# Hybrid decoder layer on one core: in the down product, the second sum's first pairs read into other tiles and in another place of the load order

## Chip, cores and metric

The kernel runs on 1 core of one Trainium2 chip. The metric is device time in microseconds (us). The kernel before has a median of 1271.38 us over three runs (1269.64 to 1272.08).

## The reference, cut to what matters

One decoder layer over 1024 tokens of width 1024: input projection, windowed attention beside a convolution branch, their gated mix, a layer norm, and then a ConvFFN. The change lies in the last matrix product, `@ ffn_w_down`, and in the start of what follows it:

```python
up = causal_dwconv(h @ ffn_w_up, ffn_dw, ffn_dw_b)
u, g = jnp.split(up, 2, axis=-1)
f = (jax.nn.gelu(g, approximate=False) * u) @ ffn_w_down
return layer_norm(DEEPNORM_ALPHA * h + f, ln2_g, ln2_b)
```

`gelu(g) * u` is 1024 x 2816 and `ffn_w_down` is 2816 x 1024, both float32.

## The kernel before, in words

**Number format.** A float32 product is computed as three passes: each operand is split into a rounded high half (a ScalarE copy, L1625) and the rest (a VectorE subtraction, L1626), and TensorE multiplies high by high, high by low and low by high.

**The up stage.** A loop over 22 chunks of 128 hidden columns computes `f`, transposed, and stores each chunk's two halves to the DRAM scratch `fd` (`f_out`, L1471 and the store behind it). The chain of the last half of a chunk is: a convolution (`conv_ffn`, L1461 to L1463), `gelu` on ScalarE (L1467), the multiplication on VectorE (L1471), the store. Temporaries of 128x512 come in rotation from eight places of the tile `FA` (`ftmp`); chunk 20 uses the first four, `FA[0:2048]`, the last chunk, 21, the next four, `FA[2048:4096]`. The tiles `c11`, `c21` and `u2` stand behind them in `FA`, `c12`, `c22` and `u13` in `OB[0:2048]`.

**The seven products.** The down product is done by Strassen and Winograd's scheme on 2 x 2 blocks: seven half-size products (the "sums" of the change's name are the accumulations), each over 11 slices of 128 hidden rows. Slices are taken in pairs, six to a product: five of two slices and one of a single slice. This document numbers the pairs 0 to 41: pairs 0 to 5 are the first product (A22 with T4, into the four accumulation banks `Z`, written `ps_z` in the profile), pairs 6 to 11 the second (A11 with B11, into `X`, `ps_x`), pairs 12 to 17 the third (S1 with T1, into `Z`), and so on. A pair of two slices is 24 matmuls of 128x512 (four banks, two slices, three passes), a single one 12. A11, A22 and A12 are blocks of `fd`; the third to sixth products read differences of blocks (S1 to S4), which lie in the DRAM scratch `sd`. `sd` is made chunk by chunk: `sums_load` reads two rows of chunks from `fd`, `sums_form` does four VectorE operations (L1501 to L1504) and stores the result in two transfers. For most chunks that happens within the up loop; the last two, 20 and 21 (`FC - 2` and `FC - 1`), are read and formed among the first pairs of the down product. Pair 16 reads what chunks 19 and 20 gave, pair 17 what chunk 21 gave. The T blocks lie in `td` and are finished long before.

**Buffers.** A pair has two raw tiles, one for the f side and one for the weight side. `F_RAW` has eight places: two in `RXF` (named `raw` in the profile), then six of 1024 columns in `FA`. `W_RAW` has six: two from a pool (`wr`), then `OB[2048:3072]`, `OB[3072:4096]`, `OB[0:1024]`, `OB[1024:2048]`. `place(i, n)` (L1608 to L1610) says which place pair i gets. The split halves of the f side have six places (`F_AT`), those of the weight side seven (`W_DN`), in rotation.

**Order.** All loads and stores of this stage are issued by SP, in program order: an instruction that waits holds up every later one. A transfer also waits for the landing of the one eight before it, because there are eight completion semaphores. `down_operands` yields pairs; `d_ahead` keeps six of them begun ahead of the product that is being emitted; `steps` (L1723) names the side work that is emitted after each pair: `gain_rows` (the norm's scale and shift rows, `w<-in_ln`), `row` (residual rows `r<-h1d`, scaled on VectorE at L1706 and L1707), `sums_load` and `sums_last`. From these a scheduler makes the order on each engine, within what `after` pins.

Of the kernel before, what the change touches and what calls it, by code (L numbers as in the profile page):

```python
# [44 lines left out]
FC = DFF // P  # L45
# [67 lines left out]
def tile_hybrid_layer(  # L113
# [9 lines left out]
    def load(o, i):  # L123
        return nc.sync.dma_start(out=o, in_=i)
# [5 lines left out]
    def f32(ap):  # L130
        return ap.bitcast(F)

    def after(ins, first):

        tc.add_manual_dep(ins.ins, first.ins.name, mybir.DependencyInfo(
            mybir.DependencyClass.NoSync, mybir.DependencyReason.SCHED_ONLY), reason="order of work")
# [159 lines left out]
    def wraw(shape):  # L296
        return wraw_p.tile(shape, F, name="wr", tag="wr")
# [479 lines left out]
    src = ps[:64, :P].rearrange("p (g d) -> p g d", d=HD)  # L777
    nc.scalar.copy(vm[:64, :, 0], src)
    nc.vector.tensor_tensor(vm[:64, :, 1], src, f32(vm[:64, :, 0]), OP.subtract)
    for q4 in range(2):  # L780
# [4 lines left out]
        src = ps[:, :].rearrange("p (n g d) -> p n g d", g=2, d=HD)  # L785
# [24 lines left out]
    for h in range(NH):  # L810
        g, r = divmod(h, 4)
        o = ps[:2, h * 16:(h + 1) * 16]
# [67 lines left out]
    for i in range(NB):  # L880
        w = 272 if i else 144
# [246 lines left out]
    for m in range(KC):  # L1128
# [38 lines left out]
        if m in (2, 3):  # L1167
            raw = (FA[:, 4112:5136], OB[:, 3072:4096])[m - 2]
# [426 lines left out]
    def blk(t, first, step, col):  # L1595
        return lambda j, n: dram(t, (first + j) * P * step + col, [[step, P], [P * step, n], [1, 512]])

    A11, A21, A12, A22 = (blk(fd, k, S, c) for k in (0, FH) for c in (0, 512))
    B11_, B12_, B21_, B22_ = (blk(w_down, k, D, c) for k in (0, FH) for c in (0, 512))
    T1, T3, T4, T2 = (blk(td, 0, 2048, q * 512) for q in range(4))  # L1600
    S2, S3, S4, S1 = (blk(sd, 0, 2048, q * 512) for q in range(4))

    F_AT = [(RHC, R_DN), (RX, 0), (RHC, 2048 + R_DN)] + [(RHO, i * 2048 + R_DN) for i in range(3)]
    W_DN = [(OC, OC_UP + i * 2048) for i in range(4)] + [(RHC, 4096 + R_DN), (RHC, 6144 + R_DN), (RHO, 6144 + R_DN)]
    F_RAW = [RXF[:, 0:1024], RXF[:, 1024:2048]] + [FA[:, i * 1024:(i + 1) * 1024] for i in range(6)]
    W_RAW = [None, None] + [OB[:, i * 1024:(i + 1) * 1024] for i in (2, 3, 0, 1)]

    def place(i, n):  # L1608

        return i % 4 if i < 6 else (i - 2) % n  # L1610
    PAIRS = [(j, min(2, FH - j)) for j in range(0, FH, 2)]

    los, evacs = [], []

    def operand(i, src, j, n, raws, places):
        raw = raws[place(i, len(raws))]
        if raw is None:
            raw = wraw([P, D])
        raw = raw[:, :n * 512]
        ins = load(raw.rearrange("p (n c) -> p n c", c=512), src(j, n))  # L1620
        after(ins, loads[-1] if loads else f_stores[-5])
        loads.append(ins)
        t, o = places[i % len(places)]
        hi, lo = (t[:, o + x:o + x + n * 512] for x in (0, 1024))
        nc.scalar.copy(hi, raw)  # L1625
        los.append(nc.vector.tensor_tensor(lo, raw, f32(hi), OP.subtract))  # L1626
        if len(los) > 1:
            after(los[-1], evacs.pop() if evacs else los[-2])
        return hi, lo

    def down_operands():
        i = 0
        for f, w in ((A22, T4), (A11, B11_), (S1, T1), (S2, T2), (S3, T3), (S4, B22_), (A12, B21_)):
            for j, n in PAIRS:
                yield (n,) + operand(i, f, j, n, F_RAW, F_AT) + operand(i, w, j, n, W_RAW, W_DN)
                i += 1

    d_stream, d_ready = down_operands(), []

    def d_ahead():  # L1640
        while len(d_ready) < 6:
            x = next(d_stream, None)
            if x is None:
                break
            d_ready.append(x)

    def d_next(ahead=True):
        if ahead:
            d_ahead()
        return d_ready.pop(0)  # L1650

    with rank(RK_SPLIT):
        d_ahead()

    def down(banks, first, done, by_tile=0, same=False):


        def mms(i, pairs, a, z):
            ops = [(p, c * 512) for p in pairs for c in range(p[0])]
            for x, ((n, fh, fl, wh, wl), o) in enumerate(ops):  # L1660
                ts, ws = slice(o + i * P, o + i * P + P), slice(o, o + 512)
                for k, (l, r) in enumerate(((fh, wh), (fh, wl), (fl, wh))):
                    nc.tensor.matmul(banks[i], l[:, ts], r[:, ws], start=first and a and x + k == 0,  # L1663
                                     stop=z and x == len(ops) - 1 and k == 2, skip_group_check=not first)

        n = len(PAIRS) - by_tile
        for y in range(n):
            p = d_next(y < 3 or not same)
            for i in range(4):
                mms(i, [p], y == 0, y == len(PAIRS) - 1)  # L1670
            if extra:
                extra.pop(0)()
        last = [d_next() for _ in range(by_tile)]
        for i in range(4):
            if last:
                mms(i, last, n == 0, True)
            with rank(RK_EVAC):
                ins = done(i)
        if same:
            evacs.append(ins)  # L1680
# [28 lines left out]
    def do(f, *x):  # L1709
        extra.append(lambda: f(*x))  # L1710
# [7 lines left out]
    def steps(*fs):  # L1718
        for f in fs:
            do(lambda f=f: [g(*x) for g, *x in f])  # L1720

    row = residual_row
    steps([(sums_load, FC - 2)], [(gain_rows, 0)], [(sums_last, FC - 2), (row, 4, 0)], [(row, 5, 0)], [(row, 6, 0)],  # L1723
          [(row, 7, 0), (sums_load, FC - 1)],
          [(row, 0, 0)], [(sums_last, FC - 1)], [(row, 1, 0)], [(row, 2, 0)], [(row, 3, 0)], [(row, 4, 1)],
          [(row, 5, 1)], [(row, 6, 1)], [(row, 7, 1)], [(row, 0, 1), (row, 1, 1)], [(row, 2, 1), (row, 3, 1)],
          [(gain_rows, 1)])
# [89 lines left out]
```

## Time and profile before

| what | value |
|---|---|
| median of three runs | 1271.38 us |
| time of the profiled execution | 1271.08 us |
| span of the profile | 1269.3 us (1.8 us of its time lie around the span) |
| TensorE granted clock over the span | 0.995 |
| VectorE, ScalarE busy | 85%, 47% |
| last matmul of the up stage to first of the down product | at 1047.4 us, without a gap |

A row of the timeline has the start in us from the span's beginning, the length, the engine, the source line, the operation, `out<-in`, shapes and a count; in brackets stands the idle time of that engine just before, and what ended it. PE is TensorE's matmul, PEld its weight load, DVE VectorE, ACT ScalarE, SPq the queue of SyncE, which issues transfers: the length of an SPq row is the time to issue, not to land. A row of several instructions spans all of them. A table by stretches gives the busy time and the count of each engine, the granted TensorE clock (1.00 is full speed), the busy share of the transfer engines and GB/s. Groups of transfers give the count, the size and the median time from issue to landing.

### The profile page before, as it was taken

To read this page: it belongs to the slowest core of one execution; us is meant where nothing else is said; L and a number is where in the kernel's file an instruction comes from. 1 tells how busy PE (TensorE), PEld (TensorE's weight loads), DVE (VectorE), ACT (ScalarE), POOL (GpSimd) and SP (SyncE) were. 2 spreads that over 40 slices of the span, in tenths; PEclk is the share of its full clock that TensorE was granted. 3 is DMA by queue.
4 is the path that set the end of the run, shared out by engine and by line. 5 is a ranking of instruction groups with operands and counts; after the bars stand their busy time and mean duration, and the time that the engine had idled before them with its cause. 6 is when DMAs were issued, how large, how long until landed. Compare 5 with 4: busy or idle time off the path is not lost.

```text
span 1269.3 us, 23031 instructions
## 1 busy us (share of the span) xinstructions
PE 1252.8 (99%) x9186; PEld 1184.5 (93%) x9186; DVE 1073.1 (85%) x1854; ACT 591.6 (47%) x1095; POOL 8.1 (1%) x9
## 2 busy tenths in 40 slices
PE   8999999999999999999999999999999999999997
PEld 7999999999999999788899999999999997788886
DVE  7888999999978577548999999998989975987697
ACT  7532355655473223335655455555554553535330
POOL 0000000001000000000000000000000000000000
PEclk9999999999999999999999999999999999999999
DMA  6375643332438364222245546454454566989712
GB/s 252 105 250 149 176 112 96 105 92 83 125 85 226 106 177 125 83 85 82 67 158 198 193 170 212 160 207 150 159 191 170 197 239 242 394 280 369 266 67 83
DMA packets 98701, 212.19 MB, mean 167 GB/s; under 512 B 11411, under 2 KB 38611, under 8 KB 98338
## 3 DMA queue, kind: packets, MB, share of 16 engines
q1 hardware_dynamic: 84474, 199.64, 47.3%
q10 hardware_dynamic: 14120, 11.08, 2.8%
q8 instruction: 72, 1.18, 0.4%
q14 instruction: 35, 0.29, 0.1%
HBM read 150.29 MB, written 62.70 MB: 168 GB/s over the span
## 4 chain that ended last, share of the span: by engine, by line
PE 93%; DVE 2%; DMA 2%; ACT 2%; issue 1%; SPq 0%; DVEq 0%; ACTq 0%
PE px L1534 14%; PE py L1534 10%; PE ps_x L1663 9%; PE ps_z L338 8%; PE ps_z L342 8%; PE ps_z L341 8%; PE pw L1534 5%; PE pz L1534 5%; PE ps_z L1663 5%; PE ps_p L342 2%; PE ps_p L338 2%; PE ps_p L341 2%; PE ps_w L342 2%; PE ps_w L338 2%; PE ps_w L341 2%; PE ps_z L556 2%
## 5 line engine op out<-in xcount | busy, mean ns | idle before, releaser
L342 PE MATMUL ps_z<-RHC,w 128*128 128x256 f32 (+2 forms) x864 | 244.6, 283 | 0.0
L338 PE MATMUL ps_z<-RHO,w 128*128 128x256 f32 (+2 forms) x864 | 244.4, 283 | 0.2 <-ACT FA L734 0.2
L341 PE MATMUL ps_z<-RHO,w 128*128 128x256 f32 (+2 forms) x864 | 243.2, 282 | 0.0
L338 PEld LDWEIGHTS ps_z<-RHO,w 128*128 128x128 f32 x864 | 162.6, 188 | 2.0 <-ACT FA L705 0.7
L341 PEld LDWEIGHTS ps_z<-RHO,w 128*128 128x128 f32 x864 | 162.7, 188 | 0.7
L342 PEld LDWEIGHTS ps_z<-RHC,w 128*128 128x128 f32 x864 | 162.7, 188 | 0.4
L725 DVE SCALAR_TENSOR_TENSOR FA<-cin,cdw,FA 128x1026 f32<-128x1026 f32 x120 | 152.3, 1279 | 0.7
L1356 DVE TENSOR_TENSOR RHO<-wr,RHO 128x512 fp32r<-128x512 f32 x94 | 63.5, 683 | 8.3 <-ACT RHO L1355 8.3
L1355 ACT CAST RHO<-wr 128x512 fp32r<-128x512 f32 x94 | 56.6, 619 | 23.2 <-DVE wr L1373 11.3
L300 ACT CAST w<-wr 128x1024 fp32r<-128x1024 f32 x37 | 38.7, 1046 | 60.8 <-PE ps_z L342 44.8
L734 ACT ACTIVATE FA<-ps_z,colr 128x258 f32<-128x258 f32 (+1 forms) x64 | 30.1, 472 | 69.8 <-PE ps_z L342 57.3
L1373 DVE TENSOR_TENSOR wr<-wr 128x512 f32<-128x512 f32 x88 | 60.0, 682 | 0.1
L303 DVE TENSOR_TENSOR w<-wr,w 128x1024 fp32r<-128x1024 f32 x37 | 45.0, 1217 | 16.3 <-ACT w L300 16.1
L1546 ACT COPY FA<-px 128x514 f32<-128x514 f32 (+2 forms) x23 | 13.1, 571 | 76.7 <-PE px L1534 76.7
L1356 DVE TENSOR_TENSOR w<-wr,w 128x512 fp32r<-128x512 f32 x60 | 40.6, 684 | 4.8 <-ACT w L1355 4.7
L1534 PE MATMUL px<-OA,RHO 128*128 128x258 f32 x324 | 43.2, 283 | 0.0
L1461 ACT ACTIVATE FA<-OB,coll 128x512 f32<-128x512 f32 x44 | 35.9, 815 | 15.0 <-DVE OB L1542 15.0
L1546 ACT COPY OB<-px 128x514 f32<-128x514 f32 (+2 forms) x46 | 26.2, 569 | 34.7 <-PE px L1534 34.5
L1534 PE MATMUL px<-RHC,RHO 128*128 128x258 f32 (+1 forms) x312 | 41.1, 281 | 0.4 <-ACT OB L1546 0.4
L1534 PE MATMUL px<-OC,RHO 128*128 128x256 f32 x324 | 41.5, 277 | 0.0
L1355 ACT CAST w<-wr 128x512 fp32r<-128x512 f32 x60 | 36.3, 618 | 11.1 <-DVE wr L1373 5.1
L1534 PEld LDWEIGHTS px<-OA,RHO 128*128 128x128 f32 x324 | 40.5, 189 | 0.2 <-ACT OB L1546 0.2
(442 smaller groups left out, 3297.2 us busy)
## 6 DMA issues: line engine op xcount, KB each, us to landing
wr<-in_w_up_dram SPq DMA_DIRECT2D x44, 512.0 KB, 3.6
wr<-in_w_z_dram SPq DMA_DIRECT2D x29, 512.0 KB, 3.7
fd<-FA SPq DMA_DIRECT2D x44, 256.0 KB, 2.1
OB<-in_w_down_dram SPq DMA_DIRECT2D x21, 512.0 KB, 4.8
FA<-sd SPq DMA_DIRECT2D x15, 512.0 KB, 9.0
qt<-qd SPq DMA_DIRECT2D x28, 256.0 KB, 4.1
sgd<-FA ACTq DMA_DIRECT2D x48, 128.0 KB, 2.7
td<-OB SPq DMA_DIRECT2D x12, 512.0 KB, 2.7
```

Source lines behind the costliest of these rows:

```text
L300: ins = nc.scalar.copy(hi, raw)
L303: return nc.vector.tensor_tensor(lo, raw, f32(hi), OP.subtract)
L338: ins = nc.tensor.matmul(ps, al, bh, start=i == 0, stop=False)
L341: nc.tensor.matmul(ps, ah, bh, start=False, stop=False)
L342: last = nc.tensor.matmul(ps, ah, bl, start=False, stop=i == n - 1)
L725: nc.vector.scalar_tensor_tensor(acc[c], cin[:, j:j + U], wc, acc[c], OP.mult, OP.add)
L1355: nc.scalar.copy(hi, src)
L1356: ins = nc.vector.tensor_tensor(lo, src, f32(hi), OP.subtract)
L1373: ins = nc.vector.tensor_tensor(*x)
L1534: ins = nc.tensor.matmul(o, x[:, ks], bmat(sub, q, hl, k), start=first and k + j == 0, stop=k == 3 and j == 2, skip_group_check=not first)
L1546: copied.append(nc.scalar.copy(*x))
L1663: nc.tensor.matmul(banks[i], l[:, ts], r[:, ws], start=first and a and x + k == 0, stop=z and x == len(ops) - 1 and k == 2, skip_group_che ...
```

## The change

`place` repeats its four places once more: pairs 6 and 7 get places 2 and 3 (`FA[0:2048]`, `OB[2048:4096]`), which pairs 2 and 3 had, in place of 4 and 5 (`FA[2048:4096]`, `OB[0:2048]`). Later pairs go round all places as before, two further on.

`operand` is cut in two: `operand_load` issues the transfer, `operand` does the split. In the list of pairs 5 and 6 change places: both are loaded when the fifth pair (pair 4) is reached, pair 6 first; then pair 6 is split before pair 5. The product still takes them by number.

In `steps`, chunk 20 is read three steps later (with residual row 5, after pair 3 instead of pair 0) and formed three steps later, after pair 5; chunk 21 is read in the same step as before and formed in the same step. The gain rows are still read in the second step, residual row 4 in the third.

```diff
     def place(i, n):

-        return i % 4 if i < 6 else (i - 2) % n
+        return i % 4 if i < 8 else (i - 4) % n
...
-    def operand(i, src, j, n, raws, places):
+    def operand_load(i, src, j, n, raws, places):
...
         loads.append(ins)
-        t, o = places[i % len(places)]
+        return raw, n, places[i % len(places)]
+
+    def operand(raw, n, at):
+        t, o = at
...
     def down_operands():
-        i = 0
-        for f, w in ((A22, T4), (A11, B11_), (S1, T1), (S2, T2), (S3, T3), (S4, B22_), (A12, B21_)):
-            for j, n in PAIRS:
-                yield (n,) + operand(i, f, j, n, F_RAW, F_AT) + operand(i, w, j, n, W_RAW, W_DN)
-                i += 1
-
-    d_stream, d_ready = down_operands(), []
+        todo = [(i,) + x for i, x in enumerate(
+            (f, w, j, n) for f, w in ((A22, T4), (A11, B11_), (S1, T1), (S2, T2), (S3, T3), (S4, B22_), (A12, B21_))
+            for j, n in PAIRS)]
+        todo[5], todo[6] = todo[6], todo[5]
+        ready = []
+
+        def begin(i, f, w, j, n):
+            ready.append((operand_load(i, f, j, n, F_RAW, F_AT), operand_load(i, w, j, n, W_RAW, W_DN)))
+
+        for x, (i, f, w, j, n) in enumerate(todo):
+            if not ready:
+                begin(*todo[x])
+            f_, w_ = ready.pop(0)
+            if x == 4:
+                begin(*todo[5])
+                begin(*todo[6])
+            yield i, (n,) + operand(*f_) + operand(*w_)
+
+    d_stream, d_ready, d_taken = down_operands(), {}, [0]

     def d_ahead():
-        while len(d_ready) < 6:
+        while len(d_ready) < (6 if d_taken[0] else 5):
             x = next(d_stream, None)
             if x is None:
                 break
-            d_ready.append(x)
+            d_ready[x[0]] = x[1]

     def d_next(ahead=True):
         if ahead:
             d_ahead()
-        return d_ready.pop(0)
+        d_taken[0] += 1
+        return d_ready.pop(d_taken[0] - 1)
...
-    steps([(sums_load, FC - 2)], [(gain_rows, 0)], [(sums_last, FC - 2), (row, 4, 0)], [(row, 5, 0)], [(row, 6, 0)],
-          [(row, 7, 0), (sums_load, FC - 1)],
+    steps([], [(gain_rows, 0)], [(row, 4, 0)], [(row, 5, 0), (sums_load, FC - 2)], [(row, 6, 0)],
+          [(row, 7, 0), (sums_last, FC - 2), (sums_load, FC - 1)],
           [(row, 0, 0)], [(sums_last, FC - 1)], [(row, 1, 0)], [(row, 2, 0)], [(row, 3, 0)], [(row, 4, 1)],
```

In the built program TensorE's order is the same instruction by instruction. On SP, pair 6's two loads now stand directly behind those of pair 4, with one `sd<-sums` store between them and one behind, ahead of the last two `fd` stores; before, they stood behind those stores, behind pair 5 and behind the two reads of chunk 20. On ScalarE pair 6's two copies now stand ahead of the last `gelu`, on VectorE its two subtractions ahead of the last multiplication of `f_out`. On SP the two reads of chunk 20 stand behind pair 8, and the four stores of chunks 20 and 21 stand together ahead of pair 16's loads; before, one stood between the two loads of pair 14, one between those of pair 15, one ahead of pair 16's and one ahead of pair 17's.

## The prediction

> **What bounds the kernel now.** I read the page's busy times first, then who waited for whom on TensorE alone, then TensorE's timeline of the down product, then a table by stretches around its one gap.
>
> ```profile
> span 1269.3 us, 23031 instructions
> PE 1252.8 (99%) x9186; PEld 1184.5 (93%) x9186; DVE 1073.1 (85%) x1854; ACT 591.6 (47%) x1095; POOL 8.1 (1%) x9
> PE ps_x L1663 <- ACT RHO L1625: 2.1, 1, 2.1
> ```
>
> TensorE is the bound: nothing but its gaps and the ends can be won. Over the whole span its longest wait is the one in the third row, in the down product, and that is the only one there.
>
> ```profile
> 1063.80 5.60 PE L1663 MATMUL ps_z<-OC,RHO 128*128 128x512 f32 x24
> 1069.23 8.32 PE L1663 MATMUL ps_z<-RHC,RHO 128*128 128x512 f32 x36
> 1079.71 7.50 PE L1663 MATMUL ps_x<-RHO,RHC 128*128 128x512 f32 x24 [2.15 <-ACT RHO L1625]
> 1080.96 5.82 PEld L1663 LDWEIGHTS ps_x<-RHO,RHC 128*128 128x128 f32 x22 [0.76 <-DVE RHO L1626]
> 1087.04 5.60 PE L1663 MATMUL ps_x<-OC,RX 128*128 128x512 f32 x24
> 1077.40:1079.70 2.30, 0.16 (x1) 0.00 (x0) 1.24 (x2) 2.02 (x2) 0.00 (x0) 0.98 1.01 393
> 1079.70:1083.10 3.40, 3.36 (x7) 2.25 (x8) 1.90 (x2) 0.50 (x1) 0.00 (x0) 0.51 1.05 389
> ```
>
> A pair of 24 matmuls takes 5.43 us from start to start (1063.80 to 1069.23; below 5.44). The 36 of pairs 4 and 5 start at 1069.23 and take 8.16, so pair 6, the first of the second product, could start at 1077.39 and pair 7 at 1082.83. They start at 1079.71 and 1087.04. The gap costs 1087.04 - 1082.83 = **4.21 us**, twice what the wait list says, in three parts: 2.32 before the first matmul; some 1.02 from 1079.94 (a matmul is 0.227) to 1080.96, for the weight side's low half; and the remaining 0.87 because the granted clock is 0.51 from 1079.70 to 1083.10 (last table row, third figure from the end).
>
> Why pair 6 is late stands in the timeline of the other engines:
>
> ```profile
> 1062.78 0.74 DVE L1463 SCALAR_TENSOR_TENSOR FA<-OB,coll,FA 128x512 f32<-128x512 f32 x1
> 1063.56 0.63 ACT L1467 ACTIVATE FA<-FA 128x512 f32<-128x512 f32 x1 [7.45 <-DVE FA L1463]
> 1064.22 0.69 DVE L1471 TENSOR_TENSOR FA<-FA 128x512 f32<-128x512 f32 x1 [0.70 <-ACT FA L1467]
> 1062.89 2.37 SPq L124 DMA_DIRECT2D fd<-FA  x2
> 1066.99 0.32 SPq L124 DMA_DIRECT2D raw<-fd  x1
> 1067.36 0.42 SPq L124 DMA_DIRECT2D wr<-td  x1
> 1067.88 0.85 SPq L124 DMA_DIRECT2D w<-fd  x2
> 1068.78 0.43 SPq L124 DMA_DIRECT2D FA<-fd  x1
> 1069.31 0.82 SPq L124 DMA_DIRECT2D OB<-in_w_down_dram  x1
> 1070.23 2.55 SPq L124 DMA_DIRECT2D w<-in_ln_dram  x2
> 1072.04 0.62 ACT L1625 CAST RHC<-wr 128x512 fp32r<-128x512 f32 x1 [1.55 <-DMA wr<-td]
> 1072.69 0.69 DVE L1626 TENSOR_TENSOR RHC<-wr,RHC 128x512 fp32r<-128x512 f32 x1 [1.48 <-ACT RHC L1625]
> 1078.61 1.04 ACT L1625 CAST RHO<-OB 128x1024 fp32r<-128x1024 f32 x1 [0.24 <-DMA OB<-in_w_down_dram]
> 1079.68 1.22 DVE L1626 TENSOR_TENSOR RHO<-OB,RHO 128x1024 fp32r<-128x1024 f32 x1
> ```
>
> SP stands still until the last `fd` store is out (its multiplication ends at 1064.91) and landed (1066.99); only then come pair 5, chunk 20 and pair 6. Pair 6's weights land at 1078.6, 11.6 us after SP went on, with 2.5 MB issued up to them (pair 5 twice 256 KB, four times 512 KB).
>
> **The change part by part.** *Pair 6's loads.* They now wait only for pair 2's subtractions, which free the raw tiles:
>
> ```profile
> 1052.18 1.22 DVE L1626 TENSOR_TENSOR RHC<-FA,RHC 128x1024 fp32r<-128x1024 f32 x1
> 1053.91 1.22 DVE L1626 TENSOR_TENSOR OC<-OB,OC 128x1024 fp32r<-128x1024 f32 x1
> 1055.06 1.05 ACT L1625 CAST RHC<-wr 128x1024 fp32r<-128x1024 f32 x1 [0.18 <-DMA wr<-td]
> 1056.00:1058.00 2.00, 2.00 (x11) 1.65 (x10) 2.00 (x3) 0.11 (x1) 0.00 (x0) 1.00 0.08 27
> sd<-sums SPq DMA_DIRECT2D x4, 512.0 KB, 3.6
> raw<-sd SPq DMA_DIRECT2D x5, 512.0 KB, 11.1
> raw<-fd SPq DMA_DIRECT2D x2, 256.0 KB, 2.9
> ```
>
> So they are issued at 1053.4 and 1055.2. A 512 KB transfer lands between 3.6 us (the lower median of this stage's groups) and 11.1 (the upper, in full queues) later. The transfer engines are nearly empty here (27 GB/s), so I take 3.6 to 4: weights in place by 1059.2. Even 11.1 would be 1066.3, against a need at 1077.39. The gap of 4.21 us goes, clock dip included.
>
> *The two copies and two subtractions ahead of the last gelu.* ScalarE is free from 1056.1 to 1063.56, so copies of 1.05 at about 1057 and 1059.2 are hidden there. If the weights land after 1062.5, the copy holds up the gelu; it costs from 1063.5 on, us for us, and with 11.1 that is 2.8. On VectorE nothing hides the subtractions: they follow the row at 1062.78. The next instruction after a 0.74 one starts 0.66 behind it (1063.44), after a 1.22 one 1.14, so they start at 1063.44 and 1064.58, and the multiplication at 1065.72 instead of 1064.22: **the last `fd` store leaves 1.50 us later**, and so do all loads that SP has behind it.
>
> *Pair 5 is late next.* Its weight half is ready at 1072.69 + 0.69 = 1073.38; 1.50 later is 1074.88. TensorE wants it at 1069.23 + 5.44 + 0.23 = 1074.90. It is just in time. Bounds: if the load lands 1.8 us sooner (2.9 us after issue, as pair 5's other load, rather than 4.7), nothing; if it is 1 us slower, 1 us of gap; with the late gelu, 2.8 more. I take 0.1, the measured landing being the same transfer in the same place.
>
> *Pair 7.* Behind the last store now stand pair 5 (0.5 MB), the gain rows (1 MB) and pair 7 (1 MB): the same 2.5 MB that stood up to pair 6's weights. So pair 7 lands 11.6 us after 1068.49, at 1080.1; the copy ends at 1081.15 and the subtraction at 1082.4. TensorE wants that at 1082.83 + 0.23 = 1083.06. Margin 0.65 us; taken as nothing, at most 1.
>
> *Later pairs and chunk 20's two reads.*
>
> ```profile
> 1082.00:1110.00 28.00, 28.00 (x123) 23.12 (x122) 26.27 (x33) 15.77 (x16) 0.00 (x0) 0.98 1.05 394
> 1106.08 1.21 DVE L1626 TENSOR_TENSOR RHC<-OB,RHC 128x1024 fp32r<-128x1024 f32 x1
> 1111.52 5.60 PE L1663 MATMUL ps_z<-RHC 128*128 128x512 f32 x24
> ```
>
> At 394 GB/s the 1.25 MB of residual row and pair 8 take 3.3 us: landed by 1083.4, ready some 3 later, wanted at 1088.3. Pair 9 stands behind 2.25 MB more, 6.0 us: landed at 1089.4, ready by 1091.8, wanted at 1093.9. From pair 10 on the queue holds 1 MB less than before (2.7 us) and starts 1.5 later: 1.2 us earlier, while TensorE comes 4.2 earlier; each margin shrinks by 3. The tightest, pair 12, is ready at 1107.29 and wanted at 1111.52: 4.2 becomes 1.2. So nothing, at most 1 us.
>
> *Sums formed later, stores together.* The row that counts is pair 17, which waits for chunk 21's store:
>
> ```profile
> 1117.27 0.39 SPq L124 DMA_DIRECT2D sd<-sums  x1
> 1124.03 0.32 SPq L124 DMA_DIRECT2D FA<-sd  x1
> 1130.78 0.69 DVE L1626 TENSOR_TENSOR OC<-OB,OC 128x512 fp32r<-128x512 f32 x1 [1.82 <-ACT OC L1625]
> 1127.84 13.76 PE L1663 MATMUL ps_z<-OC,RHO 128*128 128x512 f32 x60
> ```
>
> Pair 15 starts at 1127.84, so pair 17 is wanted at 1138.72, and 4.2 earlier now, at 1134.5. It is ready at 1131.5 even if the last store leaves no earlier than before: 3 us of cover. Without it, each us late costs one. What I expect is a store a little earlier, since chunk 21's read stands behind 1 MB less. Price nothing, at most 1.
>
> *Sum.* 1271.08 (the profiled execution, 0.30 below the median) - 4.21 + 0.1 = 1266.97; with 0.1 for the thin margins, **1267.1 us**.
>
> **A rule against the row.** The Trainium skill (TensorE: Matmul & The Clock Gate, Why this matters for your kernels) warns of idle gaps over about 3 us and names one idle window as what halves the clock. Here the clock fell to 0.51 after a gap of 2.3 us, so the measurement decides. By the rule the dip would not belong to this gap, the gain would be 0.87 us smaller, and the sum 1268.0. The dip's length, 3.4 us, agrees with the window that the same page states (What's actually happening).
>
> **Rivals.** *The gap moves to pair 5 or 7.* For it: margins of 0.02 and 0.65 us, both set by a queue that SP starts 1.5 us later. Against it: before, the same bytes landed in the times used. One case has a price: pair 5's weights land like the 7.6 us of the read behind them instead of 4.7,
>
> ```profile
> w<-fd SPq DMA_DIRECT2D x2, 512.0 KB, 7.6
> ```
>
> a 2.9 us gap and 0.87 for the clock: 1271.0. Smaller slips give 1268 to 1270.
>
> *Slower: the four stores hold up the third product.* SP issues pair 16 and 17 only behind all four stores, and pair 17 only when the last has landed (6.8 us, 1117.27 to 1124.03). Pair 17 is ready 14.2 us after that store (1117.27 to 1131.47), so it decides from a store at 1120.3 on, and the kernel is slower from one at 1123.4, with the clock's 0.87. At 1126 it is 1267.1 + 5.7 + 0.87 = 1273.7. For it: VectorE, which forms the sums, is busy 26.27 of 28.00 us above. Against it: the same operations stand in that stretch, and they would have to end 6 us later than before.
>
> *The change does not do what it says:* the first read into `FA[0:1024]` is not free at 1053.4, or what TensorE waits for in pair 6 is no transfer. Then 1271.1. The bracket in the row at 1078.61 speaks against it.
>
> **How the numbers follow.** Gap gone but for under 1 us: 0.70, 1266.0 to 1268.2 (the three runs before differ by 2.4). Gap moved: 0.20, half of it below 1268.8. Slower: 0.05. No effect: 0.05. What a measurement here can tell from no change is 0.2%, 2.5 us: faster means below 1268.8, slower above 1273.9. Faster: 0.70 + 0.10 = 0.80; same 0.10 + 0.05 = 0.15; slower 0.05. The range, 1265.8 to 1269.6, leaves out the upper part of the moved gap and the last two cases.
>
> **What would show it.** Right: no TensorE wait in the down product over 1 us, no stretch of clock 0.5 there, pair 6's copies between 1056 and 1061, pair 7 starting near 1083, the last `fd` store issued near 1066.4, pair 17's load issued before 1124. Wrong: a wait at the start of pair 5's 12 matmuls or of pair 7; a gelu after 1063.6, which says that the copy of pair 6's weights held it up; a gap in the third product behind `sd<-sums`.

## The result, and the profile after

The changed kernel takes 1266.53 us (median of seven runs, 1266.11 to 1267.68) against 1271.02 us (seven runs) of the kernel before: 0.9968 of its time, 95% interval 0.9959 to 0.9977, by that ratio faster by 4.1 us, with 2.9 to 5.2 as the interval (the two medians lie 4.5 apart). Forecast was 1267.1. The profiled execution took 1267.56 us. One run of all in this document was slow (1374.25 us, of "tiles and order alone" below): the median there includes it, the ratio leaves it out.

First the page's span, then the two rows of TensorE's wait list that lie in the down product (L1663 of before is L1679 now, L1625 is L1628, L1626 is L1629):

```profile
span 1265.8 us, 23035 instructions
PE ps_z L1679 <- DVE RHC L1629: 0.2, 1, 0.2
PE ps_z L1679 <- ACT RHC L1628: 0.2, 1, 0.2
```

The wait for pair 6 is no longer on the list. What is left stands at another place, as TensorE's timeline shows, with a stretch of the table by stretches below it:

```profile
1063.51 5.60 PE L1679 MATMUL ps_z<-OC,RHO 128*128 128x512 f32 x24
1068.95 5.60 PE L1679 MATMUL ps_z<-RHC,RHO 128*128 128x512 f32 x24
1074.73 0.50 PE L1679 MATMUL ps_z<-RHC,RHO 128*128 128x512 f32 x1 [0.18 <-ACT RHC L1628]
1075.45 2.79 PE L1679 MATMUL ps_z<-RHC,RHO 128*128 128x512 f32 x11 [0.23 <-DVE RHC L1629]
1078.08 5.60 PE L1679 MATMUL ps_x<-RHO,RHC 128*128 128x512 f32 x24
1083.52 5.60 PE L1679 MATMUL ps_x<-OC,RX 128*128 128x512 f32 x24
1256.92 0.84 PE L1679 MATMUL ps_x<-RHO 128*128 128x512 f32 x3
...
1074.00:1076.00 2.00, 1.60 (x6) 0.80 (x5) 0.69 (x1) 0.62 (x1) 0.00 (x0) 1.00 1.00 345
```

Pairs 6 and 7 follow without a pause (1078.08 to 1083.52 is 5.44), and the granted clock stays at 1.00 (third figure from the end of the last row; the stretches up to 1087 have 1.00 too). But pair 5 now comes in two pieces: one matmul at 1074.73, the other eleven from 1075.45. Pairs 4 and 5 would have ended at 1068.95 + 8.16 = 1077.11; pair 6 starts at 1078.08, so **0.97 us** is lost at pair 5.

The scatter between executions gets in the way of such small numbers, so one measure is used from here on: the time from the start of pair 3 to the start of the very last three matmuls. Before, the latter is this row of its timeline:

```profile
1260.44 0.84 PE L1663 MATMUL ps_x<-RHO 128*128 128x512 f32 x3
```

Before: 1260.44 - 1063.80 = 196.64. After: 1256.92 - 1063.51 = 193.41. Four profiles further below have no wait in between, and all give 192.44. So 4.20 us were lost before and 0.97 now. The profiled times agree to the last digit: 1271.08 - 4.20 + 0.97 - 0.29 = 1267.56, the 0.29 being pair 3's earlier start.

The other engines' timeline of after shows where pair 5 was late:

```profile
1055.21 0.37 SPq L124 DMA_DIRECT2D OB<-in_w_down_dram  x1
1060.85 1.05 ACT L1628 CAST RHO<-OB 128x1024 fp32r<-128x1024 f32 x1 [2.08 <-DMA OB<-in_w_down_dram]
1063.61 0.63 ACT L1467 ACTIVATE FA<-FA 128x512 f32<-128x512 f32 x1 [1.71 <-DVE FA L1463]
1063.50 1.22 DVE L1629 TENSOR_TENSOR RHC<-FA,RHC 128x1024 fp32r<-128x1024 f32 x1
1064.63 1.22 DVE L1629 TENSOR_TENSOR RHO<-OB,RHO 128x1024 fp32r<-128x1024 f32 x1
1065.77 0.68 DVE L1471 TENSOR_TENSOR FA<-FA 128x512 f32<-128x512 f32 x1
1068.49 0.32 SPq L124 DMA_DIRECT2D raw<-fd  x1
1068.86 1.54 SPq L124 DMA_DIRECT2D wr<-td  x1
1074.06 0.62 ACT L1628 CAST RHC<-wr 128x512 fp32r<-128x512 f32 x1 [1.84 <-DMA wr<-td]
1074.71 0.69 DVE L1629 TENSOR_TENSOR RHC<-wr,RHC 128x512 fp32r<-128x512 f32 x1 [1.77 <-ACT RHC L1628]
1079.80 1.05 ACT L1628 CAST OC<-OB 128x1024 fp32r<-128x1024 f32 x1 [0.24 <-DMA OB<-in_w_down_dram]
1080.88 1.23 DVE L1629 TENSOR_TENSOR OC<-OB,OC 128x1024 fp32r<-128x1024 f32 x1
```

Pair 6's weights are issued at 1055.21 and copied at 1060.85, when they land: ahead of the `gelu`, which comes no later for it. VectorE's two subtractions then stand ahead of the last multiplication (1065.77, was 1064.22), and SP goes on at 1068.49 (was 1066.99). Pair 5's weights leave at 1068.86 and land at 1074.0, 5.2 us later instead of 4.7. Their subtraction ends at 1075.40, half a microsecond after the forecast 1074.88, and TensorE, itself 0.28 us earlier than in the forecast, would have wanted it at 1074.62. A part of the 5.2 us is the issue: its SP row is 1.54 us long, 0.42 before.

The sums cost nothing:

```profile
1109.22 4.40 SPq L124 DMA_DIRECT2D sd<-sums  x2
1116.70 0.33 SPq L124 DMA_DIRECT2D FA<-sd  x1
1124.51 0.69 DVE L1629 TENSOR_TENSOR OC<-wr,OC 128x512 fp32r<-128x512 f32 x1
1124.32 13.76 PE L1679 MATMUL ps_z<-OC,RHO 128*128 128x512 f32 x60
```

The last store leaves at 1113.3 (the row spans both; before 1117.27), pair 17's load at 1116.70 instead of 1124.03. Pair 17 is ready at 1125.2 (the end of the third row) and wanted at 1124.32 + 10.88 = 1135.2: 10 us of cover.

### The profile page after: what moved, and what is told of

Its sections match the earlier page's. It is cut to its first block, busy times and chain, and to the rows that moved or that the text cites. A ratio compares the mean times of both kernels' runs of the same rounds, so it can differ in the third digit from the quotient of the medians.

```text
span 1265.8 us, 23035 instructions
## 1 busy us (share of the span) xinstructions
PE 1251.5 (99%) x9186; PEld 1183.6 (94%) x9186; DVE 1073.6 (85%) x1854; ACT 592.5 (47%) x1095; POOL 8.1 (1%) x9
## 4 chain that ended last, share of the span: by engine, by line
PE 87%; DVE 7%; DMA 3%; ACT 2%; issue 1%; SPq 0%; DVEq 0%; ACTq 0%
PE px L1534 12%; PE ps_x L1679 9%; PE ps_z L338 8%; PE ps_z L342 8%; PE py L1534 8%; PE ps_z L341 8%; PE ps_z L1679 5%; PE pz L1534 4%; PE pw L1534 4%; PE ps_p L342 2%; PE ps_p L338 2%; PE ps_p L341 2%; PE ps_w L342 2%; PE ps_w L338 2%; PE ps_w L341 2%; PE ps_z L556 2%
```

## The experiments

All of them in the measure of above; "lost" is the difference to 192.44. The kernels were run in groups, each beside its own runs of the kernel before, whose medians lie between 1270.10 and 1271.30; so across groups the ratios are to be compared, not the medians.

| kernel | pair 3 starts | last three matmuls | from one to the other | lost | median us | ratio to before, 95% interval |
|---|---|---|---|---|---|---|
| before | 1063.80 | 1260.44 | 196.64 | 4.20 | 1271.02 | |
| before, second profile | 1063.95 | 1260.42 | 196.47 | 4.03 | (one run: 1271.06) | |
| places alone | 1064.51 | 1261.61 | 197.10 | 4.66 | 1271.91 | 1.0004 (0.9993 to 1.0016) |
| tiles and order alone | 1064.03 | 1259.04 | 195.01 | 2.57 | 1268.69 | 0.9985 (0.9976 to 0.9995) |
| the same, 0.5 MB more | 1062.53 | 1259.19 | 196.66 | 4.22 | 1269.70 | 0.9992 (0.9984 to 1.0001) |
| steps alone | 1063.23 | 1255.73 | 192.50 | 0.06 | 1267.87 | 0.9979 (0.9970 to 0.9989) |
| steps alone, second | 1061.87 | 1255.56 | 193.69 | 1.25 | 1267.05 | 0.9970 (0.9958 to 0.9982) |
| after | 1063.51 | 1256.92 | 193.41 | 0.97 | 1266.53 | 0.9968 (0.9959 to 0.9977) |
| after, second | 1063.17 | 1256.02 | 192.85 | 0.41 | 1266.71 | 0.9968 (0.9956 to 0.9980) |
| after, third | 1064.11 | 1256.58 | 192.47 | 0.03 | 1266.98 | 0.9965 (0.9953 to 0.9978) |
| multiplication first | 1062.14 | 1254.58 | 192.44 | 0 | 1265.26 | 0.9966 (0.9952 to 0.9979) |
| multiplication first, second | 1063.60 | 1256.04 | 192.44 | 0 | 1266.71 | 0.9963 (0.9949 to 0.9976) |
| pair 5's weights early | 1062.21 | 1254.65 | 192.44 | 0 | 1266.54 | 0.9967 (0.9955 to 0.9980) |
| both remedies | 1063.41 | 1255.85 | 192.44 | 0 | 1266.59 | 0.9968 (0.9957 to 0.9980) |

### Does the gap come back, and do places alone move it?

The kernel before, profiled a second time:

> The kernel before, a second profile. My theory (the gap before pair 6 is the rule, and its size scatters with the landing of pair 6's weights by some 1 us): pair 6's weights land 11 to 12.5 us after the last store, from pair 3 to the last matmul it is 195.6 to 197.0 us, 3.2 to 4.6 above the 192.44 without a wait, with a stretch of clock 0.5 where TensorE stood still for 2.3 us or more. Rival (the first profile was an unlucky one and half of the gain of the medians lies elsewhere): below 194.5.

```profile
1069.39 8.32 PE L1663 MATMUL ps_z<-RHC,RHO 128*128 128x512 f32 x36
1079.51 1.00 PE L1663 MATMUL ps_x<-RHO,RHC 128*128 128x512 f32 x2 [1.80 <-ACT RHO L1625]
```

Lost: 4.03, as expected; TensorE stood still from 1077.71 to 1079.51, 1.80 us where the first profile has 2.15 (the 2.3 of the expectation is the first profile's wait counted from where pair 6 could have started; so counted it is 1.96 here), and the clock fell all the same (last section). The 4.20 of the prediction was no unlucky execution.

The places alone, with everything else as before:

```diff
-        return i % 4 if i < 6 else (i - 2) % n
+        return i % 4 if i < 8 else (i - 4) % n
```

> The kernel before with the new places alone (pairs 6 and 7 read into the tiles of pairs 2 and 3): load order, order of the split and list of steps as before. My theory (a place only makes an earlier load possible; where SP issues the load decides): pair 6's loads still leave behind the last store and the two reads of chunk 20, the gap before pair 6 stays at 3.2 to 4.6 us, 1271 us, within 0.2% of before. Rival (the old tiles, freed late by chunk 21, were what held the loads up): pair 6's weights land 1 us or more earlier after the last store, 1269 or less.

1271.91 us, ratio 1.0004; 4.66 us lost, slightly above the range expected. A tile that is free early is worth nothing here while the load is issued where it was. The reverse, the load order without the new places, was not run.

### The two halves of the change

New tiles and load order, old steps (against the changed kernel):

```diff
-    steps([], [(gain_rows, 0)], [(row, 4, 0)], [(row, 5, 0), (sums_load, FC - 2)], [(row, 6, 0)],
-          [(row, 7, 0), (sums_last, FC - 2), (sums_load, FC - 1)],
+    steps([(sums_load, FC - 2)], [(gain_rows, 0)], [(sums_last, FC - 2), (row, 4, 0)], [(row, 5, 0)], [(row, 6, 0)],
+          [(row, 7, 0), (sums_load, FC - 1)],
```

> The changed kernel's tiles and load order, but the old list of steps: chunk 20 is read in the first step and formed in the third. Behind the last fd store then stand pair 5 (0.5 MB), chunk 20's two reads (1 MB), the gain rows (1 MB) and pair 7. My theory (each load of the stage is as late as the bytes that SP has issued ahead of it): pair 6 starts at once behind pair 5 as in the changed kernel (gap under 0.2 us), but pair 7's weights land 1 MB, some 2.7 us, later (near 1082.5 instead of 1079.8), its low half is ready near 1084.8 and is wanted at 1083.8: a gap of about 1 us at pair 7, beside the 1 us at pair 5; 1268.5 us in a profiled execution, 1267.5 as the median. Rival A (the tiles and the load order do it all, the steps are worth nothing): no gap at pair 7, 1266.5. Rival B (the steps do nearly all of it): the old gap of 4 us comes back at pair 7, 1270.5.

TensorE's timeline, and the copy that shows when pair 7's weights land:

```profile
1069.47 5.60 PE L1679 MATMUL ps_z<-RHC,RHO 128*128 128x512 f32 x24
1075.58 0.50 PE L1679 MATMUL ps_z<-RHC,RHO 128*128 128x512 f32 x1 [0.51 <-ACT RHC L1628]
1078.90 5.60 PE L1679 MATMUL ps_x<-RHO,RHC 128*128 128x512 f32 x24
1084.48 0.49 PE L1679 MATMUL ps_x<-OC,RX 128*128 128x512 f32 x1
1085.73 5.51 PE L1679 MATMUL ps_x<-OC,RX 128*128 128x512 f32 x23 [0.77 <-DVE OC L1629]
1083.37 1.05 ACT L1628 CAST OC<-OB 128x1024 fp32r<-128x1024 f32 x1 [0.23 <-DMA OB<-in_w_down_dram]
```

Pair 6 is on time behind pair 5, as in the changed kernel, but pair 7 waits: its weights land at 1083.35, 14.7 us after SP went on (1068.68), against 11.3 in the changed kernel. One MB more ahead of it costs 3.4 us of landing (2.2 to 3.6 against the three profiles of the changed kernel). Pair 6 could have started at 1069.47 + 8.16 = 1077.63: 1.27 us are lost at pair 5, the other 1.30 at pair 7, 2.57 in all where 2 were expected; the median is 1.2 us above the expectation. Neither rival fits: the steps are worth more than nothing and less than 4 us.

The other half, old tiles and order with the new steps, applied to the kernel before:

```diff
-    steps([(sums_load, FC - 2)], [(gain_rows, 0)], [(sums_last, FC - 2), (row, 4, 0)], [(row, 5, 0)], [(row, 6, 0)],
-          [(row, 7, 0), (sums_load, FC - 1)],
+    steps([], [(gain_rows, 0)], [(row, 4, 0)], [(row, 5, 0), (sums_load, FC - 2)], [(row, 6, 0)],
+          [(row, 7, 0), (sums_last, FC - 2), (sums_load, FC - 1)],
```

> The old tiles and load order, with the new list of steps: chunk 20 is read after pair 3 and formed after pair 5, pair 6 is loaded behind pair 5 and behind the last fd store. My theory: without chunk 20's 1 MB ahead of them pair 6's weights land 2.7 us earlier than before, near 1075.9, and the low half is ready near 1078.2 where TensorE wants it at 1077.6: a gap of 0.6 us at pair 6, nothing at pair 5 (the last store leaves as early as before), no stretch of low clock; 1267.5 us profiled, 1267.0 median. So moving the two reads alone is worth some 3.6 of the 4.2 us. Rival A (without the tiles and the load order there is no gain): gap of 4 us, 1271. Rival B (the clock falls after any gap there): 0.9 us more, 1268.

> The kernel with the old tiles and load order and the new list of steps, a second time, with a second profile. In its first profile pair 6's low half was ready at about the moment TensorE wanted it. My theory (it stands on a margin of nearly nothing, so the landing of one transfer decides in each execution): the gap before pair 6 is between 0 and 1.5 us, the median 1267 to 1268, above the runs that have a real margin by 1 us or more. Rival (the steps are all that is needed, and the new tiles and load order only cost 1 us): gap of 0 to 0.1 again, and a median below that of the changed kernel in this group.

TensorE in the first of the two profiles, and in the second:

```profile
1068.67 8.32 PE L1663 MATMUL ps_z<-RHC,RHO 128*128 128x512 f32 x36
1076.83 5.66 PE L1663 MATMUL ps_x<-RHO,RHC 128*128 128x512 f32 x24
1075.72 1.23 DVE L1626 TENSOR_TENSOR RHO<-OB,RHO 128x1024 fp32r<-128x1024 f32 x1
```

```profile
1067.31 8.32 PE L1663 MATMUL ps_z<-RHC,RHO 128*128 128x512 f32 x36
1076.81 5.51 PE L1663 MATMUL ps_x<-RHO,RHC 128*128 128x512 f32 x23 [0.77 <-DVE RHO L1626]
1075.53 1.23 DVE L1626 TENSOR_TENSOR RHO<-OB,RHO 128x1024 fp32r<-128x1024 f32 x1
```

The low half of pair 6 is ready at 1076.95 and at 1076.76. In the first execution TensorE came to pair 6 at 1076.83, in the second it could have come at 1075.47: 0.06 and 1.25 us lost. 0.6 was expected; pair 6's weights land at 1074.6 in the first, 1.3 us earlier than expected, and at 1074.4 in the second, where TensorE comes to them 1.36 us sooner. So the steps alone take away most of the gap, but leave pair 6 on a margin of nothing. It is the later read that does it, not the later forming: in the kernel before, chunk 20 is formed from 1086.10 on, behind the gap, and VectorE sat idle for 5.02 us ahead of pair 6's first subtraction (1078.40). The part of the change that the prediction treated as side work thus wins more on its own by the trace (2.95 to 4.14 us) than the new tiles and order do (1.63); by the times the two halves can't be told apart (0.9979 and 0.9985 in one group). Adding tiles and order to the steps lowers the median by 0.34 us in the group that has both (1267.05 and 1266.71), less than the 1 us expected of a run with a real margin, and the intervals don't separate that.

### The rest at pair 5

The two subtractions put back behind the last multiplication (`f_mults` is a new list; the line that makes it is left out):

```diff
-        nc.vector.tensor_tensor(t, t, gate, OP.mult)
+        f_mults.append(nc.vector.tensor_tensor(t, t, gate, OP.mult))
...
             after(los[-1], evacs.pop() if evacs else los[-2])
+        if 10 < len(los) < 13:
+            after(los[-1], f_mults[-1])
```

> The changed kernel with one thing more: VectorE's two subtractions of pair 6 are put behind the last multiplication of f_out instead of ahead of it. My theory (pair 5 is late because the last store leaves 1.5 us later): the last fd store is issued near 1064.9 instead of 1066.5, pair 5's weights are issued near 1067.4 and land near 1072.3, and the gap of 0.97 us at pair 5 is gone; pair 6 stays on time; 1266.6 us profiled, 1265.6 median, 0.3 to 1 us below the changed kernel. Rival (the gap is there because pair 5's weights take 5.2 us to land, however early they are issued, and the queue is what counts): they land 5.2 us or more after their issue and at least 0.5 us of gap is left.

```profile
1061.91 0.63 ACT L1467 ACTIVATE FA<-FA 128x512 f32<-128x512 f32 x1 [1.49 <-DVE FA L1463]
1062.57 0.69 DVE L1471 TENSOR_TENSOR FA<-FA 128x512 f32<-128x512 f32 x1 [0.70 <-ACT FA L1467]
1067.58 8.32 PE L1681 MATMUL ps_z<-RHC,RHO 128*128 128x512 f32 x36
1075.74 5.60 PE L1681 MATMUL ps_x<-RHO,RHC 128*128 128x512 f32 x24
```

From the start of `gelu` to that of the multiplication it is 0.66 us here and 2.16 in the changed kernel: the 1.50 us of the prediction. Pairs 4 and 5 run as one block of 36 (8.16 us), and nothing is lost. The other remedy, pair 5's weights loaded ahead of the last two stores:

```diff
-                begin(*todo[6])
+                p, q, w5, j5, n5 = todo[6]
+                w5 = operand_load(p, w5, j5, n5, W_RAW, W_DN)
+                ready.append((operand_load(p, q, j5, n5, F_RAW, F_AT), w5))
```

> The changed kernel with one thing more: the weight side of pair 5, which comes from td and needs no store of this stage, is loaded with pair 6, ahead of the last two fd stores; its f side stays behind them. Its copy then stands ahead of the last gelu, too. My theory: pair 5's weights are in place long before 1066, its f side lands near 1071.5 and is ready near 1073, and TensorE wants it at 1074.4: no gap at pair 5, the whole 4.2 us and the 1 us are won; 1266.6 us profiled, 1265.6 median. Rival A (the f side lands as late as the weights did, near 1074): gap of 1 us stays, 1266.5 median. Rival B (the copy ahead of the gelu or the longer queue holds up the last store): the store is issued after 1066.5 by as much as is lost, 1267 or more.

```profile
1067.65 8.32 PE L1681 MATMUL ps_z<-RHC,RHO 128*128 128x512 f32 x36
```

Again a block of 36 and nothing lost; both remedies together (the two diffs above) give the same 192.44:

> The changed kernel with both single remedies: pair 5's weights loaded with pair 6, ahead of the last two fd stores, and pair 6's two subtractions behind the last multiplication. My theory (each of them alone already closes the gap at pair 5, by more than 1 us): the stretch from pair 3 to the last matmul is 192.44 again, nothing more is won; median within 0.3 us of the run with the subtractions put back, and 1 us below the changed kernel on the same chip. Rival (each alone is thin, and in other executions the gap comes back): lower than the single ones by 0.5 us or more.

The stretch is thus 0.97 us shorter than in the first profile of the changed kernel, as expected; but the medians of the three are 1265.26, 1266.54 and 1266.59, where 1265.6 was expected of the first two and 1 us below the changed kernel of the third. So the time doesn't show it clearly, and the ratios (0.9966 to 0.9968) are the changed kernel's. The changed kernel was therefore run twice more, first in the group of the third (1266.71: 0.12 above it, not 1), then beside the first:

> The changed kernel once more, on the chip of this group of runs, so that the kernels of this group have a partner. From the start of pair 3 to the start of the last matmul it took 193.41 us in its first profile; without any wait that stretch is 192.44 (before: 196.64, less the gap of 4.20). My theory (the gap at pair 5 belongs to this order and comes back in every execution): 193.0 to 193.8 again, a gap of 0.6 to 1.4 us at pair 5. Rival (it was a chance landing of one transfer): under 192.7. Median 1266 to 1267.

> The changed kernel a third time, beside the next run on the same chip. Its stretch from pair 3 to the last matmul was 193.41 and 192.85 us, with 0.97 us lost at pair 5 in one and 0.41 at pair 7 in the other. My theory now (pairs 5 and 7 both stand on margins of a few tenths, and which is late hangs on the landing of one transfer): 192.5 to 193.6 again, with a loss at pair 5, at pair 7 or at both. Rival (one of the two profiles was odd and the order has a real margin): 192.44 to 192.5.

> The kernel with pair 6's two subtractions put back behind the last multiplication, a second time. My theory (the last store 1.5 us earlier gives pairs 5 and 7 a margin above the scatter of a landing): 192.44 us from pair 3 to the last matmul again, no wait in the down product, and a median 0.3 to 1 us below the changed kernel's of the same group. Rival (its lower time was the chance of the other chip): within 0.2 us of it.

The second profile of the changed kernel, its TensorE and VectorE:

```profile
1076.77 5.60 PE L1679 MATMUL ps_x<-RHO,RHC 128*128 128x512 f32 x24
1082.21 6.01 PE L1679 MATMUL ps_x<-OC,RX 128*128 128x512 f32 x24
1088.06 5.60 PE L1679 MATMUL ps_x<-OC,RHC 128*128 128x512 f32 x24
1081.43 1.23 DVE L1629 TENSOR_TENSOR OC<-OB,OC 128x1024 fp32r<-128x1024 f32 x1
```

Here pair 5 is in time and pair 7 is late: its low half is ready at 1082.66, TensorE wanted it at 1082.21 + 0.23, and pair 8 follows 5.85 instead of 5.44 us later. In the third profile nothing is late (0.03). So 0.97, 0.41 and 0.03 us: the gap at pair 5 is not in every execution, as the second run was expected to show, and the third came out within its rival's bounds. The margins of pairs 5 and 7 are thin, but mostly hold. "Multiplication first" lost nothing in either of its profiles, but in the group that it shares with the third run of the changed kernel its median is lower by 0.27 us only (1266.71 and 1266.98), under the 0.3 expected. By the trace it has the margin that the changed kernel lacks; in time the two can't be told apart.

The reason stands in the second column of the table: pair 3 starts anywhere between 1061.87 and 1064.51. The matmul that stands one twenty-fourth of the way into the program starts between 63.4 and 65.5 us in the fourteen profiles, so 2.1 of these 2.6 us arise in the first 65 us, which no edit here touches. The times carry that scatter, the measure above doesn't.

What goes with it is the granted clock at the very start. Of the kernel before, and of "multiplication first":

```profile
11.22:14.62 3.40, 3.37 (x13) 2.79 (x14) 2.63 (x9) 2.35 (x6) 0.00 (x0) 0.50 1.02 414
11.22:14.62 3.40, 3.06 (x22) 2.44 (x20) 2.36 (x6) 3.13 (x7) 0.00 (x0) 1.00 1.01 412
```

Ten profiles have such a 3.41 us stretch at 0.50, somewhere between 10.9 and 16.3 us, and in them pair 3 starts at 1063.17 or later. In the other four (first of "multiplication first", "pair 5's weights early", second of "steps alone", and the larger dose below) it is absent, and pair 3 starts at 1062.53 or sooner. Both occur with one and the same kernel ("steps alone", "multiplication first").

### A larger dose

The run with old steps ("tiles and order alone") once more, with residual rows 4 and 5 (0.5 MB) also read ahead of pair 7; the diff is against that run:

```diff
-    steps([(sums_load, FC - 2)], [(gain_rows, 0)], [(sums_last, FC - 2), (row, 4, 0)], [(row, 5, 0)], [(row, 6, 0)],
+    steps([(sums_load, FC - 2)], [(gain_rows, 0), (row, 4, 0), (row, 5, 0)], [(sums_last, FC - 2)], [], [(row, 6, 0)],
```

> The run with the new tiles and load order and the old reads of chunk 20, with 0.5 MB more ahead of pair 7: residual rows 4 and 5 are read with the gain rows. There pair 7 was late by some 1.3 us with 2 MB between pair 5's loads and its own. My theory (lateness is the bytes issued ahead, 3.5 us for each MB as measured there): pair 7 comes 1.7 us later, a gap of 2.8 to 3.3 us. That is longer than the 2.3 us of the kernel before, after which the clock fell; so if the length of the gap is what makes it fall, the granted clock is near 0.5 for some 3.4 us behind pair 7 and 0.9 us more are lost: 1271.5 us profiled. Rival A (the clock falls for another reason than the gap): clock 1.0 behind pair 7. Rival B (small residual rows don't add to the queue): gap of 1.3 us as in that run.

TensorE's timeline, and two stretches, one ahead of the low clock and one within it:

```profile
1083.36 1.19 PE L1679 MATMUL ps_x<-OC,RX 128*128 128x512 f32 x4 [1.42 <-ACT OC L1628]
1084.97 6.42 PE L1679 MATMUL ps_x<-OC,RX 128*128 128x512 f32 x20 [0.41 <-DVE OC L1629]
1091.23 5.60 PE L1679 MATMUL ps_x<-OC,RHC 128*128 128x512 f32 x24
...
1082.03:1085.44 3.41, 1.66 (x6) 1.10 (x7) 3.41 (x6) 2.58 (x4) 0.00 (x0) 1.00 1.06 392
1086.00:1087.00 1.00, 1.00 (x4) 0.76 (x3) 1.00 (x2) 0.61 (x2) 0.00 (x0) 0.50 1.05 399
```

4.0 us are lost at pair 7 (1091.23 - 1076.35 - 10.88, pair 6 having started at 1076.35): 1.57 ahead of its first matmul, 0.70 ahead of the fifth, and 1.73 because the last twenty take 6.26 us instead of 4.53 at half the clock. So the clock does fall behind TensorE's waiting at another pair as well; with the same order and less waiting ("tiles and order alone") it stayed at 1.00. The bytes, however, were mis-sized: pair 7's weights land 15.05 us after SP goes on, only 0.4 us more than without the 0.5 MB (1.7 expected), which is nearer to what rival B says of the queue. The wait is 1.57 + 0.70 = 2.27 us, below the 2.8 to 3.3 expected and no longer than before's, and the profiled time is 1269.82, not 1271.5; so the clock's fall does not need the longer gap that the expectation built on. The wait is longer than the 1.30 without the 0.5 MB chiefly because pair 5 was late by 0.22 us here and by 1.27 there, so that TensorE came to pair 7 sooner.

## Why the prediction was right

**The gap of 4.21 us goes with its low clock.** Right: 4.20 and 4.03 lost in two profiles of before, no wait before pair 6 and no low clock in three of after. But the reason given was half of it. The prediction put the gain down to pair 6's early loads and used the later reads of chunk 20 only for the pairs behind it. The runs show two ways to close the gap before pair 6: without chunk 20's MB ahead of it, pair 6 is on time or 1.25 us late even where it was; with the new order but without the steps, pair 6 is on time, but pairs 5 and 7 are late by 2.57 us together. So the steps carry the larger part of the gain. The three parts of the 4.21 were also cut wrongly: 22 weight loads follow 1080.96 in the prediction's row, so two matmuls, not one, ran before it. The wait for the low half is then 1080.96 - 1079.71 - 2 x 0.227 = 0.80 us, and the low clock costs 1.09 (22 matmuls take 6.08 us instead of 4.99), not 0.87. The sum is untouched by that; the time without the low clock's share of the gain would be 1268.2, not 1268.0.

**Pair 6's landing.** Taken as 3.6 to 4 us, measured 5.6 (1055.21 to 1060.8), within the bounds and hidden, as forecast. `gelu` starts at 1063.61 (1063.56 before), by 0.01 past the 1063.6 that was to be a sign of a late copy; its bracket names VectorE's convolution, which ends 0.05 later here, and not the copy.

**The last store 1.50 us later.** Right to 0.05: the multiplication moved from 1064.22 to 1065.77, SP's next load to the forecast 1068.49.

**Pair 5 just in time: the term of the sum that was mis-sized.** 0.1 us taken, 0.97, 0 and 0.03 measured. A wait at the start of pair 5 was named as a sign of being wrong, and in the first profile it is there, in small. The price rested on one landing of 4.7 us, where the landings of that same transfer are 3.8, 4.5 and 5.2 in the three profiles of after. The bound "1 us slower, 1 us of gap" held.

**Pair 7, margin 0.65, nothing taken.** Its weights were put at 11.6 us after SP goes on; the three profiles have 11.3, 12.5 and 11.1. In the second the margin was used up and 0.41 us lost. The rival in which the gap moves to pair 5 or 7 thus happened in small, at most 0.97 of its 2.9 us.

**Pair 12 and the sums.** Nothing taken, nothing lost: pair 12 is ready at 1104.52 and wanted at 1108.00, 3.5 us of margin where 1.2 was forecast; pair 17 has 10 us of cover, and the rival with the four stores is out by that much.

**The sum.** 1266.97 for the profiled execution without the 0.1 of thin margins, and 1267.56 measured: 0.87 more at pair 5, 0.29 less ahead of pair 3. That the median came within 0.6 us of the forecast is in part luck, as pair 3's start alone scatters by 2.6 us among the profiles.

**The rule that spoke for 1268.0.** TensorE stood still for 2.15 us before, 1.80 in its second profile, 2.16 + 0.53 with places alone and 1.42 + 0.41 in the larger dose, and each time the clock fell; with old steps and new order it stood still for 0.51 + 0.22 ahead of pair 5 and 0.77 at pair 7, and the clock stayed up. The Trainium skill (TensorE: Matmul & The Clock Gate, What's actually happening) describes a free-running window of 3413 ns; the rows of the last section agree with that. The same page's advice (Why this matters for your kernels) warns of idle gaps over about 3 us only; here 1.80 us was enough. That the dip belonged to the gap, and its cost to the gain, was right.

## What to carry to other kernels

Where a load is late, count the bytes that its queue has issued ahead of it before moving its buffer: putting another transfer behind it can be worth as much as moving it forward (here 2.95 to 4.14 us of 4.20), and leaves the order of the copies and subtractions alone. Work that is pulled ahead of a store's producer delays every load that waits for that store, so pin it behind. A margin below the scatter of a landing (here over 1 us) is none: look at more than one profile before a gap of that size enters a sum.

## What was not expected of the hardware

The low clock comes in one fixed length, and not at once. The granted clock is 0.50 from 1079.59 to 1083.00 before, 1079.80 to 1083.21 in its second profile, 1081.25 to 1084.66 with places alone and 1085.44 to 1088.85 in the larger dose: 3.41 us each time, starting 2.0 to 3.5 us after TensorE came to a stop, in three of the four after it had set to work again. And it comes on a grid: in each of the fourteen profiles the times at which the granted clock changes lie whole multiples of 3.413 us apart (before: 4.39, 11.21, 14.63, 1079.59, 1083.00 and 1263.91; from the third to the fourth it is 312 times 3.4133). What counts is then the 3.41 us ahead of a fall. The first row is the kernel before ahead of 1079.59, the second "multiplication first" early in the program, where the clock did not fall (PE busy is the second figure):

```profile
1076.17:1079.58 3.41, 1.39 (x7) 0.81 (x5) 1.18 (x1) 2.02 (x2) 0.00 (x0) 1.00 1.03 402
7.15:10.56 3.41, 1.65 (x15) 1.41 (x13) 2.77 (x10) 2.40 (x4) 0.00 (x0) 1.00 1.01 405
```

TensorE was busy for 1.39 us in the first, and for 1.60, 1.15 and 1.66 ahead of the other three falls; in the run with old steps, whose gaps left the clock at 1.00, it was busy for 2.65 us and more of each such stretch. In other parts of these programs the clock stayed at 1.00 behind stretches of the grid with 1.65 us (the second row) and with 1.82 to 2.45 us. These rows fit a rule by the busy share of a stretch of the grid, with a limit near one half, and not one by the length of an unbroken pause: one of 2.05 us early in "pair 5's weights early" (ended at 10.92, across a line of the grid) left the clock at 1.00, one of 1.80 us did not. The limit is no sharper than that: 1.65 stayed and 1.66 fell, and the ends of matmuls are modelled in a profile. Where on the grid a pause falls differs from execution to execution, which would also make the early fall of some profiles a matter of chance; that was not tested. Two pauses of 1.42 and 0.41 us can cost more in clock (1.73) than one of 2.15 whose low stretch is partly spent waiting (1.09).

A transfer's time to land is not a matter of its bytes alone: pair 5's 256 KB took 3.8 to 5.8 us from its issue in the seven profiles of the new load order that load it there, and 1 MB more ahead of pair 7 cost 3.4 us, 0.5 MB in two pieces 0.4. A part of it is the issue itself: in the three of the seven in which pair 5's SP row is 1.5 us long it took 4.5 to 5.8 us, in the four in which it is 0.42 us long 3.8 to 4.7. What decides the rest was not separated.
